# A four-mixer decoder block in split fp32: squares on GpSimd, moved value weights, a third half in two splits, a last block in unequal stores

## The chip, the cores and the metric

The kernel runs on one core of a Trainium2 chip. The metric is the device time of one execution in microseconds (us). A profiled execution shows the engines: TensorE (PE, with its weight loads as PEld), VectorE (DVE), ScalarE (ACT), GpSimd (POOL), and SyncE (SP), which here only starts DMAs.

## What is computed

One decoder layer on 256 tokens of width 2048, all in fp32:

```
h = rms_norm(x);  [qA|kA|vA|qB|kB|vB|qC|kC|vC] = h @ w_in       # 2048 x 6144
x = x + concat(diff_attention_A, moba_B, dilated_C) @ w_out     # 6 + 4 + 6 heads of 128
x = x + memory_cross_attention(rms_norm(x), rms_norm(mem), w_cq, w_ckv, w_co)
g, u = split(rms_norm(x) @ w_up);  g = causal_conv3(g) + conv_b
x = x + (silu(g) * u) @ w_down                                  # 2048 -> 2 x 5632 -> 2048
out = rms_norm(x)                                               # times g_final
```

`rms_norm(x)` is `x * rsqrt(mean(x * x) + 1e-6) * g`. Its sum of squares is what the change moves to another engine at the first norm.

## The kernel before, in words

x is kept transposed: 16 blocks of 128 features by 256 tokens in `xin`. Each fp32 operand of a large product is split into a high part, rounded to fp32r, and a low part (the rest), and a product is high x high + high x low + low x high. The norm's factor is applied after the product, so `hT` (x times the gain, high and low side by side, 512 columns a block) can be made at once and the sum of squares comes later.

Weights stream from HBM in **pieces** of 1 MB (`raw`, 4 buffers). A piece has two **halves** of 128 x 1024. For each half ScalarE copies the high part (`hi<-raw`, L142) and VectorE subtracts (`lo<-raw,hi`, L149); `hi` and `lo` have 5 buffers each. A half is split four halves ahead of its use; from the fifth buffer on, the split waits until TensorE is through with the buffer's last half. TensorE works half by half, in program order:

- `wstat_chunk`: a chunk of 512 output features, 8 halves. Weights are the stationary operand and `hT` moves: for each of 4 groups of 128 features and 2 blocks, a matmul of 512 columns (L295, high weights) and one of 256 (L302, low weights). A half has 8 such pairs. The four sums lie in four PSUM banks of the tag `acc`, which has 5. At the end `merge` (L354, L355) copies one side with ScalarE and adds the other with VectorE into `mg`; this frees the bank.
- `astat_chunk`: values for attention. Here the weights move (512 or 256 columns) and `hT` is stationary: L341, L342, L343.
- `down`: w_down, also with moving weights (L851, L852, L853). The last two of its 44 pieces wait until all else is summed and are then taken block by block of 512 output columns, so that a block's norm work lies beside the next block's matmuls.

Nothing schedules by itself: instructions stand on each engine in the order in which the code is written. `before(i, f)` and `after(i, f)` hang a piece of work ahead of or behind the matmuls of half i.

At the start SyncE and ScalarE issue the loads of x and of the first pieces in small parts, by turns (`load_x`, `load_block`, `load_half`); TensorE runs 24 transposes meanwhile. The squares of x are taken by ScalarE in four parts of 1024 columns (`square_part`, L223, after halves 5 to 8) and added by VectorE (L227). `norm_factors(10, "x")` folds them on VectorE ahead of half 10's splits (L236) and sums over partitions on TensorE behind half 10 (L241).

At the end (`down`, k = 43) each of the two token tiles goes block by block: add the sums to x (L900, L902), square and sum on ScalarE (L265), multiply by the gain (L873). Then the factor `rfin` (GpSimd, L915) scales: `finish` (L862 to L868) uses ScalarE, VectorE or GpSimd, and SyncE stores (L869). Block 3 of the second tile is split in two halves of 256 columns, the second in a bank of its own.

Of the kernel before, what the change touches and what calls it, by code (L numbers as in the profile page):

```python
# [20 lines left out]
NT = 2  # L21
# [41 lines left out]
def trunk(ctx, tc, x, mem, w_in, w_out, diff_lambda, rel_bias_table, w_cq, w_ckv, w_co, w_up, conv, w_down,  # L63
# [34 lines left out]


    class Piece:  # L100
        def __init__(self, srcs, mm, extra=None):
            self.srcs, self.mm, self.extra = srcs, mm, extra
            self.raw = None
            self.parts = [None, None]

# [25 lines left out]
    def load_half(p, h):  # L131
# [4 lines left out]
                       ap=[list(src.ap[0]), [src.ap[1][0], k], list(src.ap[2])])  # L136
        SP.dma_start(p.raw[:, h * HALF:(h + 1) * HALF].rearrange("p (k n) -> p k n", k=k), half)

    def split_hi(p, h):
        hi = wpool.tile([P, HALF], F32R, tag="hi", name="hi", bufs=NSPLIT)  # L140
        lo = wpool.tile([P, HALF], F32R, tag="lo", name="lo", bufs=NSPLIT)
        ACT.copy(hi, p.raw[:, h * HALF:(h + 1) * HALF])  # L142
        p.parts[h] = (hi, lo)
        if p.extra is not None and h == 0:
            p.extra[0]()
# [61 lines left out]
    def xblock(k):  # L207
        return xT[:, k, :]
# [5 lines left out]
    def square_part(i, key, c, src):  # L214

        st = {}

        def square():
            tag, bufs = ("v", 2) if key == "x" else ("sq", 1) if c else ("sqsum", 2)
            st["t"] = t = pools["att"].tile([P, NT, 512], F32, tag=tag, name="sq", bufs=bufs).rearrange("p t n -> p (t n)")  # L220
            if not c:
                squares[key] = t
            ACT.activation(t, src(), AF.Square)  # L223

        after(i, square)
        if c:
            before(i + 1, lambda: DVE.tensor_tensor(squares[key], squares[key], st["t"], op=ALU.add))  # L227
# [51 lines left out]
    def wstat_chunk(w, col0, src, evac, korder=tuple(range(KD)), bank=acc_tile, wide=True):  # L279


        accs = [None] * 4
        last = len(korder) // 4 - 1

        def mm(pi):
            def f(p, h):
                hi, lo = (a.rearrange("p (k n) -> p k n", k=2) for a in p.parts[h])
                if pi == 0 and h == 0:
                    accs[:] = [bank() for _ in range(4)]

# [13 lines left out]

                if cur[0] <= 2:
                    for f in (high, low):
                        for j in range(2):
                            for n in range(4):
                                f(n, j)
                    return  # L310
                for n in range(4):
                    for j in range(2):
                        high(n, j)
                        low(n, j)
                    if pi == last and h == 1:
                        evac(n, accs[n])
            return f

        for pi in range(last + 1):
            pieces.append(Piece(sources(w, korder[4 * pi:4 * pi + 4], col0, 512), mm(pi)))  # L320

    def astat_chunk(w, col0, ncol, src, evac, korder):

        accs = [None] * NT
        nk = 2 * HALF // ncol
        nkh = nk // 2
        last = len(korder) // nk - 1

        def mm(pi):
            def f(p, h):  # L330
                hi, lo = (a.rearrange("p (k n) -> p k n", k=nkh) for a in p.parts[h])
                for t in range(NT):
                    if pi == 0 and h == 0:
# [12 lines left out]
            return f  # L346

        for pi in range(last + 1):
            pieces.append(Piece(sources(w, korder[pi * nk:(pi + 1) * nk], col0, ncol), mm(pi)))

    def merge(a):

# [493 lines left out]
    def down_mm(p, k, h, t, n, c0=0, c1=512, own=None):  # L846
        hi, lo = p.parts[h]
        ah, al = (a[:, t * P:(t + 1) * P] for a in parts[k])
        o, first = (outs[t, 2 * h + n][:, c0:c1], 0) if own is None else (own, KF - TAIL)
        wh, wl = (a[:, n * 512 + c0:n * 512 + c1] for a in (hi, lo))  # L850
        PE.matmul(o, ah, wh, start=(k == first), stop=False)  # L851
        PE.matmul(o, ah, wl, start=False, stop=False)  # L852
        PE.matmul(o, al, wh, start=False, stop=(k == KF - 1))  # L853

    ss3 = small(10, "ss3", 1)
    fin = {}

    def finish(n, t, og, r):
        col = slice(n * 512, (n + 1) * 512)
        if t:  # L860
            if n < 2:
                ACT.activation(og[:, col], og[:, col], AF.Copy, scale=r)  # L862
            else:
                DVE.scalar_tensor_tensor(og[:, col], xtok(t, n), r, gfin["t"][:, col], op0=ALU.mult, op1=ALU.mult)
        elif n < 2:
            ACT.activation(og[:, col], og[:, col], AF.Copy, scale=r)
        else:
            POOL.tensor_scalar_mul(og[:, col], og[:, col], r)  # L868
        SP.dma_start(out[t * P:(t + 1) * P, col], og[:, col])  # L869

    def gained(og, t, n):
        col = slice(n * 512, (n + 1) * 512)
# [2 lines left out]
    def down(k):  # L875
        def f(p, h):
# [8 lines left out]
                        down_mm(p, k, h, t, n)  # L885
            elif k == KF - 1 and h == 1:
                done = None
                for t in range(NT):
                    og = wpool.tile([P, 2 * HALF], F32, tag="raw", name="raw", bufs=NRAW)
                    ms = small(2, "msf")  # L890
# [1 line left out]

                    parts_of = ((0, 0, 512), (1, 0, 512), (2, 0, 512)) + (((3, 0, 256), (3, 256, 512)) if t else ((3, 0, 512),))
                    for i, (n, c0, c1) in enumerate(parts_of):
                        own = any_tile()[:, :c1 - c0] if c0 else None
                        for kk in range(KF - TAIL, KF):
                            down_mm(fin[kk], kk, n // 2, t, n % 2, c0, c1, own)
                        xc = xtok(t, n)[:, c0:c1]
                        if own is None:
                            DVE.tensor_tensor(xtok(t, n), outs[t, n], xtok(t, n), op=ALU.add)  # L900
                        else:
                            DVE.tensor_tensor(xc, own, xc, op=ALU.add)  # L902
                        square_sum(xc, ss[:, i:i + 1], c1 - c0)
                        if done:
                            for m in ((2, 0), (3, 1), (), (), ())[i]:
                                finish(m, *done)
                        if not t or n < 2:
                            gained(og, t, n)
                    DVE.reduce_sum(ms[:, 0:1], ss[:, :3], axis=AX.X)
                    DVE.tensor_scalar(ms[:, 0:1], ms[:, 0:1], 1.0 / D, EPS, op0=ALU.mult, op1=ALU.add)  # L910
# [3 lines left out]
                    r = small(1, "rfin")  # L914
                    POOL.tensor_tensor(r, ms[:, 1:2], mhalf, op=ALU.pow)  # L915
                    done = t, og, r
                for n in (2, 0, 3, 1):
                    finish(n, *done)
        return f

    for k in range(KF):
# [20 lines left out]
                      bass.AP(tensor=src.tensor, offset=src.offset + k * src.ap[1][0],  # L942
                              ap=[list(src.ap[0]), list(src.ap[2])]))

    load_x(0, 2)
    load_block(ACT, pieces[0], 0)
    load_block(SP, pieces[0], 1)
    ACT.copy(small(1, "first", 1), mhalf)
    load_x(2, 2)
    load_half(pieces[0], 1)  # L950
    load_x(4, 2)
    load_half(pieces[1], 0)
    load_x(6, 2)
# [16 lines left out]
                f(xblock(k + j), MIX, lambda: hT["h"], k + j)  # L970

    def split(i):
        split_hi(pieces[i // 2], i % 2)
        split_lo(pieces[i // 2], i % 2)

    put_x(0)
    p = pieces[0]
    p.parts[0] = hi, lo = [wpool.tile([P, HALF], F32R, tag=t, name=t, bufs=NSPLIT) for t in ("hi", "lo")]
    for j in range(2):
        c = slice(j * 512, (j + 1) * 512)  # L980
        ACT.copy(hi[:, c], p.raw[:, c])
        DVE.tensor_tensor(lo[:, c], p.raw[:, c], hi[:, c].bitcast(F32), op=ALU.subtract)
    put_x(2)
    split(1)
    load(pieces[3])
    nload = 4

    for i in range(3):
        for j in range(2):
            after(i, lambda h=2 * i + j: (put_x(2 * h + 4), split(h + 2)))  # L990
    for c in range(4):
        square_part(c + 5, "x", c, lambda c=c: xpart(c))
    norm_factors(10, "x")
    mixed["t"] = buf1.tile([P, KD, 2 * S], F32R, tag="hT", name="hT")

# [85 lines left out]
```

## Time and profile before

| | us |
|---|---|
| median of 3 runs (1243.31 to 1245.57) | 1243.32 |
| the profiled execution's own time | 1244.53 |
| its span (first to last instruction) | 1242.7 |
| TensorE busy | 1229.7 |
| VectorE busy | 830.9 |
| ScalarE busy | 630.3 |
| GpSimd busy | 14.2 |

Times in the profile count from the span's start. A matmul's duration runs over the start of the next one, since matmuls are pipelined: the pace is read from the starts, the durations serve to compare equal shapes.

### The profile page before, as it was taken

The numbers are of one execution on the slowest core, as the hardware profiler recorded it, in microseconds if no ns is written. First come the engines' busy times: TensorE is split into PE (matmuls) and PEld (weight loads), VectorE is DVE, ScalarE is ACT, GpSimd is POOL, SyncE is SP. The second block draws the span as 40 slices with busy tenths as digits, with TensorE's granted clock in tenths as the row PEclk, the third lists the DMA queues.
The fourth block names the chain that finished last, engine by engine and source line by source line (L and its number), as shares of the span: only waits on it lengthen the run. The fifth ranks groups of instructions, "written<-read, shape, count | busy, mean of one in ns | idle before, by whom it ended". The sixth has DMA issues, their size and how long they took to land.

```text
span 1242.7 us, 17626 instructions
## 1 busy us (share of the span) xinstructions
PE 1229.7 (99%) x6934; PEld 1072.0 (86%) x6934; DVE 830.9 (67%) x1351; ACT 630.3 (51%) x981; POOL 14.2 (1%) x23
## 2 busy tenths in 40 slices
PE   8999999999999999999999999999999999999997
PEld 7888888988888899888888888888888888888885
DVE  7755667567568877776767768767677755554555
ACT  7445656556455656545444445444444544444444
POOL 0000000000000000000000000000000000000001
PEclk9999999999999999999999999999999999999998
DMA  9665554555566555565565565565656555555541
GB/s 345 209 195 190 175 178 163 184 168 173 177 216 218 170 169 166 202 206 173 169 203 183 190 198 178 182 203 190 197 176 203 185 188 204 180 192 203 180 160 68
DMA packets 104835, 233.26 MB, mean 188 GB/s; under 512 B 4208, under 2 KB 14768, under 8 KB 98992
## 3 DMA queue, kind: packets, MB, share of 16 engines
q1 hardware_dynamic: 104576, 231.85, 55.7%
q8 instruction: 54, 0.88, 0.3%
q10 hardware_dynamic: 144, 0.26, 0.1%
q14 instruction: 29, 0.24, 0.1%
q0 software_dynamic: 32, 0.02, 0.0%
HBM read 230.00 MB, written 2.12 MB: 187 GB/s over the span
## 4 chain that ended last, share of the span: by engine, by line
issue 58%; PE 37%; DVE 2%; DMA 1%; ACT 0%; POOL 0%; SPq 0%; POOLq 0%; DVEq 0%; ACTq 0%
PE acc L295 16%; PE acc L302 8%; PE acc L341 3%; PE acc L343 3%; PE acc L342 3%; DMA raw<-in_w_in 1%; PE at L401 1%; DVE lo L149 1%; PE at L420 0%; DMA xin<-in_x 0%; PE at L444 0%; PE acc L298 0%; PE acc L297 0%; DVE hT L197 0%; PE at L472 0%
## 5 line engine op out<-in xcount | busy, mean ns | idle before, releaser
L149 DVE TENSOR_TENSOR lo<-raw,hi 128x1024 fp32r<-128x1024 f32 x423 | 517.2, 1224 | 352.5 <-ACT hi L142 352.0
L142 ACT CAST hi<-raw 128x1024 fp32r<-128x1024 f32 x423 | 443.1, 1049 | 465.6 <-PE acc L295 273.3
L295 PE MATMUL acc<-hT,hi 128*128 128x512 f32 x1776 | 624.8, 394 | 2.5 <-DVE mg L355 1.9
L302 PE MATMUL acc<-hT,lo 128*128 128x256 f32 x1840 | 511.7, 280 | 0.0
L295 PEld LDWEIGHTS acc<-hT,hi 128*128 128x128 f32 x1776 | 334.0, 188 | 77.1 <-DVE mg L355 2.2
L302 PEld LDWEIGHTS acc<-hT,lo 128*128 128x128 f32 x1840 | 345.2, 188 | 0.3
L295 PE MATMUL at<-hT,hi 128*128 128x512 f32 x528 | 187.5, 392 | 0.0
L302 PE MATMUL at<-hT,lo 128*128 128x256 f32 x528 | 147.6, 280 | 0.0
L295 PEld LDWEIGHTS at<-hT,hi 128*128 128x128 f32 x528 | 99.2, 188 | 21.8
L302 PEld LDWEIGHTS at<-hT,lo 128*128 128x128 f32 x528 | 99.1, 188 | 0.0
L851 PE MATMUL acc<-hi,ah 128*128 128x512 f32 (+1 forms) x222 | 87.0, 392 | 0.0
L853 PE MATMUL acc<-hi,al 128*128 128x512 f32 (+1 forms) x222 | 86.6, 390 | 0.0
L852 PE MATMUL acc<-lo,ah 128*128 128x512 f32 (+1 forms) x222 | 85.7, 386 | 0.0
L341 PE MATMUL acc<-hi,hT 128*128 128x256 f32 (+1 forms) x224 | 75.0, 335 | 0.0
L343 PE MATMUL acc<-hi,hT 128*128 128x256 f32 (+1 forms) x224 | 73.9, 330 | 0.0
L342 PE MATMUL acc<-lo,hT 128*128 128x256 f32 (+1 forms) x224 | 73.8, 330 | 0.0
L788 ACT ACTIVATE y<-y 128x256 f32<-128x256 f32 x44 | 18.5, 419 | 66.4 <-DVE y L784 66.3
L851 PE MATMUL at<-hi,ah 128*128 128x512 f32 x132 | 52.0, 394 | 0.0
L853 PE MATMUL at<-hi,al 128*128 128x512 f32 x132 | 51.7, 392 | 0.0
L852 PE MATMUL at<-lo,ah 128*128 128x512 f32 x132 | 51.2, 388 | 0.0
L853 PEld LDWEIGHTS acc<-hi,al 128*128 128x128 f32 x222 | 41.7, 188 | 9.6
L852 PEld LDWEIGHTS acc<-lo,ah 128*128 128x128 f32 x222 | 41.7, 188 | 9.2
(159 smaller groups left out, 1005.0 us busy)
## 6 DMA issues: line engine op xcount, KB each, us to landing
raw<-in_w_up SPq DMA_DIRECT2D x88, 1024.0 KB, 5.1
raw<-in_w_in SPq DMA_DIRECT2D x45, 1024.0 KB, 5.2
raw<-in_w_down SPq DMA_DIRECT2D x44, 1024.0 KB, 4.9
raw<-in_w_out SPq DMA_DIRECT2D x12, 1024.0 KB, 5.2
raw<-in_w_ckv SPq DMA_DIRECT2D x8, 1024.0 KB, 5.3
raw<-in_w_out SPq DMA_DIRECT2D x8, 512.0 KB, 4.8
raw<-in_w_cq SPq DMA_DIRECT2D x4, 1024.0 KB, 5.3
raw<-in_w_co SPq DMA_DIRECT2D x4, 1024.0 KB, 5.3
```

The source lines that it names most:

```text
L142: ACT.copy(hi, p.raw[:, h * HALF:(h + 1) * HALF])
L149: DVE.tensor_tensor(lo, p.raw[:, h * HALF:(h + 1) * HALF], hi.bitcast(F32), op=ALU.subtract)
L295: PE.matmul(accs[n], w, x, start=(i == 0), stop=False)
L302: PE.matmul(accs[n][:, :S], lo[:, j, n * P:(n + 1) * P], src()[:, korder[i], :S], start=False, stop=(i == len(korder) - 1))
L341: PE.matmul(o, xh, hi[:, j, :], start=(i == 0), stop=False)
L342: PE.matmul(o, xh, lo[:, j, :], start=False, stop=False)
L343: PE.matmul(o, xl, hi[:, j, :], start=False, stop=(i == len(korder) - 1))
L401: PE.matmul(out, a[u], b[w], start=first and i == 0, stop=last and i == 2)
L788: after(cur[0] + 1 + n, lambda: ACT.activation(gate[k], gate[k], AF.Silu))
L851: PE.matmul(o, ah, wh, start=(k == first), stop=False)
L852: PE.matmul(o, ah, wl, start=False, stop=False)
L853: PE.matmul(o, al, wh, start=False, stop=(k == KF - 1))
```

## The change

Six things are changed.

1. **Squares of x.** The four squares of the first norm and their three additions become `POOL.tensor_tensor`, issued ahead of everything but the first setup. ScalarE and VectorE no longer have them.
2. **Rows of `hi` and `lo`.** Each buffer gets rows of 1280 elements instead of 1024. Value weights (`astat_chunk`) lie 56 elements (224 bytes) into the row, the others at its start. The room comes from a smaller DMA scratch, 4096 bytes instead of 16384, and so every tile lies elsewhere in SBUF.
3. **The start.** x's first two blocks are loaded one by one, the second half of the first piece in two loads, and the first two halves are split block by block; the third half's split is done in two parts of 512 columns.
4. **The order of the first half's matmuls.** Block 0 high and low, then block 1, instead of both highs first.
5. **The end, before the last block.** VectorE adds the sums of the second tile's block 3 without the last two pieces to x ahead of time, and both halves of that block get banks of their own.
6. **The last scalings and stores.** VectorE takes block 1 instead of ScalarE. The second tile's four stores have 256, 512, 768 and 512 columns instead of 512 each.

```
-        hi = wpool.tile([P, HALF], F32R, tag="hi", name="hi", bufs=NSPLIT)
-        lo = wpool.tile([P, HALF], F32R, tag="lo", name="lo", bufs=NSPLIT)
+        return [wpool.tile([P, HALF + 256], F32R, tag=t, name=t, bufs=NSPLIT)[:, p.shift:p.shift + HALF] for t in ("hi", "lo")]
...
-            pieces.append(Piece(sources(w, korder[pi * nk:(pi + 1) * nk], col0, ncol), mm(pi)))
+            pieces.append(Piece(sources(w, korder[pi * nk:(pi + 1) * nk], col0, ncol), mm(pi), shift=56))
...
+                DVE.tensor_tensor(xtok(1, 3), outs[1, 3], xtok(1, 3), op=ALU.add)
...
-                for n in (2, 0, 3, 1):
-                    finish(n, *done)
+                for n, c0, c1, send in ((2, 0, 256, 0), (0, 0, 512, 0), (2, 256, 512, None), (3, 0, 512, -256), (1, 0, 512, 0)):
+                    finish(n, *done, c0, c1, send)
...
-    load_x(0, 2)
+    load_x(0, 1)
     load_block(ACT, pieces[0], 0)
+    load_x(1, 1)
     load_block(SP, pieces[0], 1)
     ACT.copy(small(1, "first", 1), mhalf)
     load_x(2, 2)
-    load_half(pieces[0], 1)
+    load_block(SP, pieces[0], 2)
+    load_block(SP, pieces[0], 3)
...
-        square_part(c + 5, "x", c, lambda c=c: xpart(c))
+        t = pools["att"].tile([P, NT, 512], F32, tag="v", name="sq", bufs=2).rearrange("p t n -> p (t n)")
+        POOL.tensor_tensor(t, xpart(c), xpart(c), op=ALU.mult)
+        if c:
+            POOL.tensor_tensor(squares["x"], squares["x"], t, op=ALU.add)
...
-    nc = bacc.Bacc("TRN2", target_bir_lowering=False, num_devices=1)
+    nc = bacc.Bacc("TRN2", target_bir_lowering=False, num_devices=1, dynamic_dma_scratch_size=4096)
```

**Where instructions move.** VectorE around the first merges, before (`lo` are splits, `sq` squares, `mg` merges, each row with its line and the size of what it writes):

```order
16 L149 TENSOR_TENSOR lo<-raw,hi 128x1024 x4
17 L227 TENSOR_TENSOR sq<-sq 128x1024
18 L149 TENSOR_TENSOR lo<-raw,hi 128x1024
19 L355 TENSOR_TENSOR mg<-acc,mg 128x256 x4
20 L227 TENSOR_TENSOR sq<-sq 128x1024
21 L149 TENSOR_TENSOR lo<-raw,hi 128x1024
22 L227 TENSOR_TENSOR sq<-sq 128x1024
```

and the same place after the change:

```order
20 L152 TENSOR_TENSOR lo<-raw,hi 128x1024 x5
21 L358 TENSOR_TENSOR mg<-acc,mg 128x256 x4
22 L152 TENSOR_TENSOR lo<-raw,hi 128x1024 x2
23 L239 TENSOR_TENSOR sq<-sq 128x512
24 L239 TENSOR_TENSOR sq<-sq 128x256
```

The additions of squares are gone from VectorE; the folds of 512 and 256 columns stay and now read what GpSimd wrote. GpSimd's row from its last setup instruction (`ident`) to the first norm factor (`rcol_x`), after the change:

```order
10 masks.py:199 AFFINE_SELECT ident<-ident 128x128
11 L1024 TENSOR_TENSOR sq<-xin 128x1024 x2
12 L1026 TENSOR_TENSOR sq<-sq 128x1024
13 L1024 TENSOR_TENSOR sq<-xin 128x1024
14 L1026 TENSOR_TENSOR sq<-sq 128x1024
15 L1024 TENSOR_TENSOR sq<-xin 128x1024
16 L1026 TENSOR_TENSOR sq<-sq 128x1024
17 L193 TENSOR_TENSOR rcol_x<-ms_483,mhalf 128x2
```

Before, rows 11 to 16 were not there. VectorE at the very end, after the change (`xin<-acc` and `xin<-at` are sums, `msf` the norm's scalars, `raw` holds the result):

```order
994 L907 TENSOR_TENSOR xin<-at,xin 128x512
995 L868 TENSOR_SCALAR raw<-raw,rfin 128x512
996 L907 TENSOR_TENSOR xin<-at,xin 128x512
997 L907 TENSOR_TENSOR xin<-acc,xin 128x256 x2
998 L914 TENSOR_REDUCE msf<-ss_92 128x1
999 L915 TENSOR_SCALAR msf<-msf 128x1
1000 L917 SCALAR_TENSOR_TENSOR msf<-ss_92,msf 128x1
1001 L918 SCALAR_TENSOR_TENSOR msf<-ss_92,msf 128x1
1002 L864 SCALAR_TENSOR_TENSOR raw<-xin,rfin,gfin 128x256 x2
1003 L864 SCALAR_TENSOR_TENSOR raw<-xin,rfin,gfin 128x512 x2
```

Before, row 995 was the product with the gain, row 997 an addition of 512 columns and one of 256, and the last scalings were two of 512.

## Rows read from the trace of the kernel before

**Rows 1.** The page's head: span, then busy time, share, instructions.

```profile
span 1242.7 us, 17626 instructions
PE 1229.7 (99%) x6934; PEld 1072.0 (86%) x6934; DVE 830.9 (67%) x1351; ACT 630.3 (51%) x981; POOL 14.2 (1%) x23
```

**Rows 2.** Stretches: length, busy (instructions) by engine, granted clock, DMA share, GB/s.

```profile
31.50:34.85 3.35, 3.35 (x11) 2.87 (x12) 3.35 (x6) 1.87 (x2) 0.00 (x0) 0.50 1.01 334
```

**Rows 3.** Timeline of TensorE: start, length, line, operation, operands, [idle before <-releaser].

```profile
6.21 0.96 PE L295 MATMUL acc<-hT,hi 128*128 128x512 f32 x3 [0.64 <-DVE hT L197]
...
28.63 0.39 PE L295 MATMUL acc<-hT,hi 128*128 128x512 f32 x1
...
28.97 0.39 PE L295 MATMUL acc<-hT,hi 128*128 128x512 f32 x1
...
31.36 0.71 PE L295 MATMUL acc<-hT,hi 128*128 128x512 f32 x1 [1.88 <-DVE mg L355]
...
32.08 0.63 PE L295 MATMUL acc<-hT,hi 128*128 128x512 f32 x1
```

**Rows 4.** Timeline of VectorE ahead of the first merges.

```profile
23.85 4.85 DVE L149 TENSOR_TENSOR lo<-raw,hi 128x1024 fp32r<-128x1024 f32 x4
28.62 1.22 DVE L227 TENSOR_TENSOR sq<-sq 128x1024 f32<-128x1024 f32 x1
29.75 1.22 DVE L149 TENSOR_TENSOR lo<-raw,hi 128x1024 fp32r<-128x1024 f32 x1
30.89 1.41 DVE L355 TENSOR_TENSOR mg<-acc,mg 128x256 f32<-128x256 f32 x4
```

**Rows 5.** Timeline of ScalarE in the start phase.

```profile
10.81 0.91 ACT L194 ACTIVATE hT<-xin 128x256 fp32r<-128x256 f32 x2
...
20.83 1.05 ACT L142 CAST hi<-raw 128x1024 fp32r<-128x1024 f32 x1 [2.69 <-DMA raw<-in_w_in]
...
25.45 1.06 ACT L223 ACTIVATE sq<-xin 128x1024 f32<-128x1024 f32 x1
26.41 1.03 ACT L142 CAST hi<-raw 128x1024 fp32r<-128x1024 f32 x1
```

**Rows 6.** Groups by shape: count, then busy us, mean ns, idle us before.

```profile
L302 PE MATMUL acc<-hT,lo 128*128 128x256 f32 x1840 | 511.7, 280 | 0.0
...
L851 PE MATMUL acc<-hi,ah 128*128 128x512 f32 x218 | 85.9, 394 | 0.0
...
L852 PE MATMUL acc<-lo,ah 128*128 128x512 f32 x218 | 84.6, 388 | 0.0
...
L341 PE MATMUL acc<-hi,hT 128*128 128x512 f32 x96 | 38.6, 402 | 0.0
...
L342 PE MATMUL acc<-lo,hT 128*128 128x512 f32 x96 | 37.8, 393 | 0.0
L341 PE MATMUL acc<-hi,hT 128*128 128x256 f32 x128 | 36.4, 284 | 0.0
L342 PE MATMUL acc<-lo,hT 128*128 128x256 f32 x128 | 36.1, 282 | 0.0
```

**Rows 7.** Timeline of GpSimd at the end.

```profile
1230.85 3.59 POOL L868 TENSOR_SCALAR raw<-raw,rfin 128x512 f32<-128x512 f32 x2
1235.55 0.57 POOL L915 TENSOR_TENSOR rfin<-msf,mhalf 128x1 f32<-128x1 f32 x1 [1.12 <-DVE msf L913]
```

**Rows 8.** Timeline of VectorE at the end.

```profile
1224.79 0.69 DVE L873 TENSOR_TENSOR raw<-xin,gfin 128x512 f32<-128x512 f32 x1
...
1232.09 0.69 DVE L873 TENSOR_TENSOR raw<-xin,gfin 128x512 f32<-128x512 f32 x1
...
1236.16 1.41 DVE L864 SCALAR_TENSOR_TENSOR raw<-xin,rfin,gfin 128x512 f32<-128x512 f32 x2 [0.69 <-POOL rfin L915]
```

**Rows 9.** Timeline of TensorE: the column sums of the squares.

```profile
40.66 0.50 PE L241 MATMUL at<-ones,sq 128*128 128x1 f32 x4
```

**Rows 10.** The same view as Rows 2, for the last stores.

```profile
1237.75:1240.00 2.25, 0.00 (x0) 0.00 (x0) 0.00 (x0) 0.00 (x0) 0.00 (x0) 0.50 1.03 351
```

More of the change, by code (lines that the diff above doesn't have):

```diff
@@ L100, in trunk, with __init__ @@
     class Piece:
-        def __init__(self, srcs, mm, extra=None):
-            self.srcs, self.mm, self.extra = srcs, mm, extra
+        def __init__(self, srcs, mm, extra=None, shift=0):
+            self.srcs, self.mm, self.extra, self.shift = srcs, mm, extra, shift
             self.raw = None
@@ L137, in load_half, with part_tiles @@
         SP.dma_start(p.raw[:, h * HALF:(h + 1) * HALF].rearrange("p (k n) -> p k n", k=k), half)
+    def part_tiles(p):
+        return [wpool.tile([P, HALF + 256], F32R, tag=t, name=t, bufs=NSPLIT)[:, p.shift:p.shift + HALF] for t in ("hi", "lo")]
     def split_hi(p, h):
-        hi = wpool.tile([P, HALF], F32R, tag="hi", name="hi", bufs=NSPLIT)
-        lo = wpool.tile([P, HALF], F32R, tag="lo", name="lo", bufs=NSPLIT)
+        hi, lo = part_tiles(p)
         ACT.copy(hi, p.raw[:, h * HALF:(h + 1) * HALF])
@@ L218, in square @@
         def square():
-            tag, bufs = ("v", 2) if key == "x" else ("sq", 1) if c else ("sqsum", 2)
+            tag, bufs = ("sq", 1) if c else ("sqsum", 2)
             st["t"] = t = pools["att"].tile([P, NT, 512], F32, tag=tag, name="sq", bufs=bufs).rearrange("p t n -> p (t n)")
@@ L305, in f @@
                 if cur[0] <= 2:
[L306 to L309, printed above, removed]
+                    for j, f in (((0, high), (0, low), (1, high), (1, low)) if cur[0] == 0 else
+                                 ((0, high), (1, high), (0, low), (1, low))):
+                        for n in range(4):
+                            f(n, j)
                     return
@@ L852, in down_mm, with finish @@
         PE.matmul(o, ah, wl, start=False, stop=False)
-        PE.matmul(o, al, wh, start=False, stop=(k == KF - 1))
+        PE.matmul(o, al, wh, start=False, stop=k == KF - 1 or (own is None and (t, 2 * h + n, k) == (1, 3, KF - TAIL - 1)))
     ss3 = small(10, "ss3", 1)
     fin = {}
[L858 to L865, printed above, removed]
+    def finish(n, t, og, r, c0=0, c1=512, send=0):
+        col = slice(n * 512 + c0, n * 512 + c1)
+        if t and n:
+            DVE.scalar_tensor_tensor(og[:, col], xtok(t, n)[:, c0:c1], r, gfin["t"][:, col], op0=ALU.mult, op1=ALU.mult)
+        elif n == 0:
             ACT.activation(og[:, col], og[:, col], AF.Copy, scale=r)
+        elif n == 1:
+            DVE.tensor_scalar_mul(og[:, col], og[:, col], r)
         else:
             POOL.tensor_scalar_mul(og[:, col], og[:, col], r)
-        SP.dma_start(out[t * P:(t + 1) * P, col], og[:, col])
+        if send is not None:
+            col = slice(n * 512 + send, n * 512 + c1)
+            SP.dma_start(out[t * P:(t + 1) * P, col], og[:, col])
     def gained(og, t, n):
@@ L894, in f @@
                     for i, (n, c0, c1) in enumerate(parts_of):
-                        own = any_tile()[:, :c1 - c0] if c0 else None
+                        own = any_tile()[:, :c1 - c0] if (t, n) == (1, 3) else None
                         for kk in range(KF - TAIL, KF):
@@ L899, in f @@
                         if own is None:
-                            DVE.tensor_tensor(xtok(t, n), outs[t, n], xtok(t, n), op=ALU.add)
-                        else:
-                            DVE.tensor_tensor(xc, own, xc, op=ALU.add)
+                            own = outs[t, n][:, c0:c1]
+                        DVE.tensor_tensor(xc, own, xc, op=ALU.add)
                         square_sum(xc, ss[:, i:i + 1], c1 - c0)
@@ L906, in f @@
                                 finish(m, *done)
-                        if not t or n < 2:
+                        if not t or n < 1:
                             gained(og, t, n)
@@ L972, in split, with put_high, put_low @@
     def split(i):
+        if i == 2:
+            p = pieces[1]
+            p.parts[0] = hi, lo = part_tiles(p)
+            for c in (slice(0, 512), slice(512, HALF)):
+                ACT.copy(hi[:, c], p.raw[:, c])
+                DVE.tensor_tensor(lo[:, c], p.raw[:, c], hi[:, c].bitcast(F32), op=ALU.subtract)
+            return
         split_hi(pieces[i // 2], i % 2)
         split_lo(pieces[i // 2], i % 2)
-    put_x(0)
+    def put_high(k):
+        high(xblock(k), MIX, lambda: hT["h"], k)
+    def put_low(k):
+        low(xblock(k), MIX, lambda: hT["h"], k)
     p = pieces[0]
[L978 to L984, printed above, removed]
+    for h in range(2):
+        p.parts[h] = hi, lo = part_tiles(p)
+        if h:
+            put_high(2)
+            put_high(3)
+        for j in range(2):
+            k = 2 * h + j
+            c = slice(j * 512, (j + 1) * 512)
+            r = p.raw[:, h * HALF + j * 512:h * HALF + (j + 1) * 512]
+            if h == 0:
+                put_high(k)
+            n = 2 if k == 0 else 1
+            for i in range(n):
+                w = 512 // n
+                ACT.copy(hi[:, j * 512 + i * w:j * 512 + (i + 1) * w], r[:, i * w:(i + 1) * w])
+            put_low(k)
+            DVE.tensor_tensor(lo[:, c], r, hi[:, c].bitcast(F32), op=ALU.subtract)
     load(pieces[3])
@@ L991, in trunk @@
     for c in range(4):
-        square_part(c + 5, "x", c, lambda c=c: xpart(c))
+        t = pools["att"].tile([P, NT, 512], F32, tag="v", name="sq", bufs=2).rearrange("p t n -> p (t n)")
+        POOL.tensor_tensor(t, xpart(c), xpart(c), op=ALU.mult)
+        if c:
+            POOL.tensor_tensor(squares["x"], squares["x"], t, op=ALU.add)
+        else:
+            squares["x"] = t
     norm_factors(10, "x")
```

## The prediction

> **What bounds the kernel now.** I read the page's busy line first, then the queries by stretch and by time for the start and the end, then the groups of matmuls by shape. TensorE is busy 1229.7 of 1242.7 us [rows 1]; the reader is to see that a microsecond on VectorE, ScalarE or GpSimd counts only where TensorE waits for it, and that there are three ways to gain: shorter matmuls, fewer waits, a shorter end. The waits are nearly all in one place. At 28.97 us a pair of matmuls starts, pairs follow each other every 0.34 us, and the next one starts at 31.36, so 31.36 - 28.97 - 0.34 = 2.05 us are lost [rows 3]. The next pair takes 0.72 instead of 0.34 us, since the granted clock is 0.50 (the 1.2 GHz level) for the 3.35 us behind the pause [rows 2, 3]: half of 3.35, 1.7 us, is lost again. Together 3.7 us.
>
> What TensorE waits for there is an accumulator of the first chunk, freed by VectorE's `mg` additions. They start at 30.89, behind four splits (23.85 on), an addition of squares (28.62) and another split (29.75), one closely after the other [rows 4]. On ScalarE two squares of 1.06 us stand among the casts that these splits need [rows 5].
>
> **The change part by part.**
>
> *Squares on GpSimd.* ScalarE loses four squares, VectorE three additions of 1.22 us. VectorE's row before the merges is then five splits and no addition: the fifth split takes the addition's place at 28.62, the first merge the place of the split at 29.75, 1.14 us ahead of 30.89 [rows 4]. TensorE went on at 31.36 and so goes on 1.14 earlier, at 30.22; it wants the bank at 29.31, so 0.9 us of the wait stay. The casts are no hindrance: without the square of 25.45 the cast of 26.41 can only come earlier [rows 5]. Whether the clock drops behind a wait of 0.9 us is not shown; the one of 0.64 at 6.21 was followed by matmuls at full pace, three in 0.96 us [rows 3], so I take it that it does not, and the 1.7 are won too. Sum -2.8; bounds -3.7 (no wait at all) and -1.1 (the clock drops just the same), and on the other side the first two rivals below.
>
> *The price on GpSimd.* Seven operations of 128x1024 with two inputs. The nearest rows: two of 128x512 with one input took 3.59 us, 1.8 each, of which 0.57 is about what an operation on one column takes [rows 7]. So 1024 columns cost 0.57 + 2 x 1.23 = 3.0 us if the second input is free, and 5.5 if it costs as much as the first. I take 3.5. Six of the seven come after blocks 4 to 7 of x, the last of which ScalarE reads at 10.81 [rows 5], so the sum is ready near 10.8 + 6 x 3.5 = 32. VectorE folds it in two additions (some 1.2 us, by 0.69 for 512 columns [rows 8] and half as many more), and TensorE's column sums, in order behind the eleventh half, come at 40.66 now [rows 9] and 2.8 us earlier then, at 37.9: 36.7 less the fold. The limit is (36.7 - 10.8) / 6 = 4.3 us an operation. Cost 0 with that cover. VectorE's new wait at the fold holds back splits of halves that TensorE reads four halves later, so it alone costs nothing.
>
> The Trainium skill ("GPSIMD Engine Reference", section 3.1, Elementwise) gives 4497 ns for an addition of 2048 columns of fp32; an estimate from it is some 2.3 to 2.5 us for 1024, with which the sum would be ready near 26 us; no run here shows it yet.
>
> *Finer loads and another order at the start.* TensorE's first real matmul, at 6.21 [rows 3], can come some 0.7 us earlier, since the first block of x is sent alone. But ScalarE waits until 20.83 for the weights of the seventh half [rows 5], its cast of 1.05 and its split of 1.2 end near 23.1, and TensorE is there already: 6.21 + 6 halves of 8 pairs at 0.345 = 22.8. The bytes ahead of that load are the same, so what is won at 6 us is waited for at 23. I take 0; bounds -0.3 and +0.5 (the stepwise order, with casts of one block that TensorE waits for one by one).
>
> *Value weights.* 288 matmuls of 512 columns and 384 of 256 (96 and 128 on each of three lines [rows 6]). The 512s last 402 ns on L341 and 393 on L342 (L343 is like L342), 396 on the mean; those of w_down, of equal shape but at other places in SBUF, 394 and 388 on L851 and L852 (L853 lies between them), 391 on the mean: 288 x 5 ns = 1.4 us. The 256s last 284 and twice 282, against 280 on L302: 2.7 x 384 = 1.0. If the moved rows run like the others, 2.4 us are won; I take 2.0, since the 402 holds some matmuls that followed a pause. No row shows a matmul on weights 224 bytes further. Bounds: all like L852 (388), -3.4; all like L341, +2.1. The other weights keep their place in a row, but rows get 1024 bytes longer and every buffer lies elsewhere; the three lines of w_down differ by 6 ns with nothing but operands to tell them apart, so 1056 of them could go 3 ns either way, 3.2 us. I take 0.
>
> *The end.* The first half of the last block no longer waits for an addition over 512 columns, and ScalarE has one scaling less between its sums: the last sum comes 0.2 us sooner. VectorE scales all but one quarter: 1.41 us for two of 512 columns now [rows 8], with two of 256 more about 2.3, so its last product is ready 0.7 later. But the stores, not the products, set the end: from 1237.75 to 1240 the queues move 351 GB/s, DMA share 1.03 [rows 10], and a first store of 128 KB can go 0.3 us sooner. About -0.5; bounds -1.0 (all of 0.2 and 0.3, and no gap) and +0.7 (the last store waits for VectorE). The first block's new VectorE scaling shares its time with GpSimd's and is within these bounds.
>
> **Sum.** -2.8 - 2.0 - 0.5 = -5.3. The profiled execution took 1244.53 us (span 1242.7 and 1.8 around it), so 1239.2 for it; the median of the three runs before lies 1.2 lower, at 1243.32, hence the forecast of 1238.0.
>
> **Rivals.**
>
> *GpSimd holds VectorE back (slower).* Both read SBUF, and every split has two SBUF inputs. If a GpSimd operation keeps the path until it ends, each split that meets one waits. In the stretch from 23.85 on, where VectorE has hardly a gap [rows 4], GpSimd would be at work all the time; two or three waits of 3 us each stand ahead of the merges. TensorE then waits 0.9 us and that delay, the clock falls for 1.7, and what is won elsewhere is 2.5: at two waits 0.9 + 6 + 1.7 - 3.7 - 2.5 = +2.4, 1245.7; at three 1248.7. It decides from a delay of 3.6 us. Against it: at 1232.09 VectorE multiplied two SBUF tensors in 0.69 us, while GpSimd's first scaling had run since 1230.85, and the same product alone, at 1224.79, also took 0.69 [rows 7, 8]. The Trainium skill ("SBUF — State Buffer", Who interferes with whom) has this rule, an exclusive lock in which the one that comes second blocks fully; by it the trace disagrees on VectorE's side, in this one instance. Chance 0.10.
>
> *The squares come late.* Past 4.3 us an operation TensorE waits at the column sums: at 5.5 the sum is ready at 43.8, a wait of 7.1 us and 1.7 for the clock, against 5.3 won: 1246.8. From 4.9 us on it is slower than before. For it: the bounds 3.0 and 5.5 lie on either side of the limit. Chance 0.12, two thirds of it slower, the rest no change.
>
> *Most of it given back (no change).* The clock drops behind the shorter wait, so the start gives 1.1, or 0.5 if GpSimd slows the splits a little; the values keep their 393 to 402 ns, and the end gives 0.3: 1242.0 to 1242.5. For it: no row shows the new place of the values, or a wait of 0.9 us in full work. Against it: the full pace behind the wait at 6.21 [rows 3]. Chance 0.18, a quarter of it faster by a little over 0.2%.
>
> **How the numbers follow.** The forecast has 0.60, with its own range 1235.2 to 1240.6 (start -1.6 to -3.7, values -1.0 to -3.4, end -0.1 to -1.0, all ends together left out). What a measurement can tell here is 0.2%, 2.5 us. Faster 0.60 + 0.04 = 0.64; slower 0.10 + 0.08 = 0.18; no change 0.18. The range that leaves out two in ten: 1234.4 (beyond it the unshown gain of w_down) to 1244.5 (beyond it the first two rivals).
>
> **What would show it.** Right: no idle stretch over 1 us on TensorE between 28 and 32 us and a granted clock of 1.00 through 35; the first `mg` addition near 29.75; GpSimd's last addition before 36 us; splits still at 1.22 us; L344 to L346 (the old L341 to L343) near 391 and 280 ns; the last store's data complete some 0.5 us sooner after the last matmul. Wrong: splits that last or wait over 2 us between 10 and 35 us (the first rival); TensorE idle before the column sums (the second); value matmuls at 393 to 402 as before, or w_down's durations changed (my terms of 2.0 and 0).

## The result, and the profile after

| | us | against the kernel before |
|---|---|---|
| forecast | 1238.0 (1234.4 to 1244.5) | faster |
| kernel before, 4 runs beside it | 1244.05 (1243.31 to 1245.57) | |
| changed kernel, 4 runs | 1252.15 (1251.75 to 1252.86) | ratio 1.0067, interval 1.0052 to 1.0082 |

The change made the kernel slower by 0.5 to 0.8%; the forecast had the wrong sign, and the time lies outside its range. Two executions far outside all others, 4752.02 us of the kernel before and 1454.63 us of the run with the squares one half later in it, are left out of every comparison below. The span grew from 1242.7 to 1250.0 us. The page's head after, with its busiest row of matmuls (columns as in [rows 1] and, for the last line, group | busy, mean ns | idle before, releaser):

```profile
span 1250.0 us, 17646 instructions
...
PE 1230.7 (98%) x6934; PEld 1072.7 (86%) x6934; DVE 841.4 (67%) x1353; ACT 626.5 (50%) x978; POOL 30.3 (2%) x30
...
L305 PE MATMUL acc<-hT,lo 128*128 128x256 f32 x1840 | 512.6, 280 | 7.5 <-DVE lo L152 4.5
```

TensorE did as many matmuls in nearly the same busy time [rows 1]; what grew is idle time, from 13.0 to 19.3 us, and one group has 7.5 of it, on VectorE's account. GpSimd has 30.3 us instead of 14.2. VectorE is busier by 10.5 us although three additions of 1.22 us went away: its instructions lasted longer.

To find the place, I compared the start of each matmul in the two traces (both have 6934). The changed kernel is 0.05 us ahead at the first real one, 12.9 us late at the hundredth, 9.2 late at the column sums (49.86 us; 40.66 before [rows 9]), still 9.2 late at the first value matmul, 7.9 at the last, 8.0 at the kernel's last matmul, 7.3 at the span's end. So the start lost 9.2, the values gave 1.3, the end gave 0.8. All of the loss falls between 7 and 30 us. VectorE there (start, length, line, operation, operands, [idle before]; several rows left out):

```profile
7.15 2.03 DVE L200 SCALAR_TENSOR_TENSOR hT<-xin,hT 128x256 fp32r<-128x256 f32 x1
9.11 0.68 DVE L1014 TENSOR_TENSOR lo<-raw,hi 128x512 fp32r<-128x512 f32 x1
...
10.71 2.51 DVE L200 SCALAR_TENSOR_TENSOR hT<-xin,hT 128x256 fp32r<-128x256 f32 x2
13.14 5.15 DVE L985 TENSOR_TENSOR lo<-raw,hi 128x512 fp32r<-128x512 f32 x2
18.21 4.60 DVE L200 SCALAR_TENSOR_TENSOR hT<-xin,hT 128x256 fp32r<-128x256 f32 x2
22.74 3.35 DVE L152 TENSOR_TENSOR lo<-raw,hi 128x1024 fp32r<-128x1024 f32 x1
...
26.81 1.21 DVE L152 TENSOR_TENSOR lo<-raw,hi 128x1024 fp32r<-128x1024 f32 x1
```

and GpSimd:

```profile
6.75 2.15 POOL L1024 TENSOR_TENSOR sq<-xin 128x1024 f32<-128x1024 f32 x1 [5.40 <-DMA xin<-in_x]
10.73 2.20 POOL L1024 TENSOR_TENSOR sq<-xin 128x1024 f32<-128x1024 f32 x1 [1.83 <-DMA xin<-in_x]
13.01 2.43 POOL L1026 TENSOR_TENSOR sq<-sq 128x1024 f32<-128x1024 f32 x1
...
22.61 2.40 POOL L1026 TENSOR_TENSOR sq<-sq 128x1024 f32<-128x1024 f32 x1
```

The reader is to lay the two lists on one axis. A split of 512 columns takes 0.68 us at 9.11 and 2.6 at 13.14, a split of 1024 takes 3.35 at 22.74 and 1.21 at 26.81. GpSimd is at work from 10.73 to 25.01 almost without a gap, and in that time VectorE gets one operation through for each of GpSimd's. With the one at 7.15 that makes seven, and together they last 12.9 us longer than usual. Before 10.73 (but for 7.15, beside GpSimd's first) and after 25.01 every length is the usual one. TensorE's waits, each on what VectorE was late with:

```profile
16.05 0.73 PE L305 MATMUL acc<-hT,lo 128*128 128x256 f32 x4 [1.52 <-DVE lo L985]
...
18.35 0.73 PE L305 MATMUL acc<-hT,lo 128*128 128x256 f32 x4 [1.57 <-DVE lo L985]
...
20.93 0.77 PE L298 MATMUL acc<-hT,hi 128*128 128x512 f32 x1 [1.85 <-DVE hT L200]
...
26.15 0.58 PE L305 MATMUL acc<-hT,lo 128*128 128x256 f32 x1 [4.45 <-DVE lo L152]
```

And the clock (columns as in [rows 2]):

```profile
5.00:14.10 9.10, 8.99 (x48) 7.38 (x47) 8.98 (x11) 8.06 (x17) 5.44 (x3) 1.00 1.03 386
...
19.53:29.77 10.24, 4.39 (x13) 3.42 (x14) 10.24 (x9) 2.79 (x4) 5.33 (x3) 0.50 0.47 154
```

During the third of those waits the granted clock fell to 0.50 (the 1.2 GHz level) for 10.24 us. From start to start the four steps are 1.91, 1.84, 2.12 and 5.22 us where one matmul's step is about 0.2: 10.2 us lost. From 26.15 to 29.77 TensorE works at half pace, which costs another 1.8. With the 0.5 it was late by 14 us already, that makes 12.5 of the 12.9. The pause and half clock that the kernel before had near the first merges [rows 2, 3] no longer occur, and the lag falls from 12.9 to 9.2: TensorE comes there that much later, and VectorE has caught up (its two splits ahead of the merges wait 1.08 and 1.55 us for their casts).

### The profile page after: what moved, and what is told of

Same layout as the page of the kernel before. It is cut to its first block, busy times and chain, and to the rows that moved or that the text cites. A ratio compares the mean times of both kernels' runs of the same rounds, so it can differ in the third digit from the quotient of the medians.

```text
span 1250.0 us, 17646 instructions
## 1 busy us (share of the span) xinstructions
PE 1230.7 (98%) x6934; PEld 1072.7 (86%) x6934; DVE 841.4 (67%) x1353; ACT 626.5 (50%) x978; POOL 30.3 (2%) x30
## 3 DMA queue, kind: packets, MB, share of 16 engines
HBM read 230.00 MB, written 2.12 MB: 186 GB/s over the span
## 4 chain that ended last, share of the span: by engine, by line
issue 58%; PE 38%; DVE 2%; DMA 1%; POOL 0%; SPq 0%; ACT 0%; POOLq 0%; DVEq 0%; ACTq 0%
PE acc L298 16%; PE acc L305 9%; PE acc L344 3%; PE acc L346 3%; PE acc L345 3%; DMA raw<-in_w_in 1%; PE at L404 1%; DVE lo L152 1%; DVE hT L200 1%; PE at L423 0%; PE at L447 0%; PE acc L301 0%; PE acc L300 0%; PE at L475 0%; POOL raw L870 0%
```

## The experiments

Two theories stood after this reading. A: GpSimd's operations hold VectorE's back, whoever needs their result. B: the finer loads and the stepwise splits of the start cost it. "Lag" below is how much later TensorE starts the column sums (or their half) than at 40.66 us in the kernel before; a ratio is that of the times, with its interval. The profiled execution that gives the 40.66 has the half clock of [rows 2], 1.7 us by the prediction's sum; and one kernel profiled twice, the changed kernel with its squares one half later (below), has lags of -0.5 and -1.8. So a lag of one or two microseconds decides nothing.

**The squares back.** The changed kernel, its squares on ScalarE and VectorE as before:

```
-        POOL.tensor_tensor(t, xpart(c), xpart(c), op=ALU.mult)
...
+        square_part(c + 5, "x", c, lambda c=c: xpart(c))
```

> The changed kernel with the four squares back on ScalarE and their additions on VectorE, as in the kernel before; all else as changed. Theory A (GpSimd's two-input operations hold VectorE's splits back): the 9.2 us that the start lost are gone, the pause ahead of the first merges is back, so the start stands within 0.5 us of the kernel before; the values keep 1.2 and the end 0.7 us: about 1.9 us under the kernel before, near 1242.1. Theory B (the finer loads and the stepwise splits of the start cost it): the start stays some 9 us late, near 1252. VectorE's splits of 1024 columns last 1.22 us under A, over 2 us under B.

1241.44 us, ratio 0.9990 (0.9980 to 0.9999); lag -1.1 us, splits at 1.22 us. Six of its ten executions took 1241.21 to 1241.45 us, four 1242.51 to 1243.03. A holds, B falls: before the first merges TensorE is 0.6 us behind the kernel before, and 0.5 and 0.6 us in two runs below that have the old loads and splits ("by itself" and "one input"), so the new ones cost nothing that can be told.

**The squares alone.** The kernel before with only the squares moved:

```
-        square_part(c + 5, "x", c, lambda c=c: xpart(c))
+        POOL.tensor_tensor(t, xpart(c), xpart(c), op=ALU.mult)
...
```

> The kernel before with nothing but the squares and their additions on GpSimd. Theory A (GpSimd's two-input operations hold VectorE's splits back): the column sums come some 9 us later than in the kernel before, as in the changed one, and the time is near 1253 to 1254. Theory B (the finer loads and the stepwise splits cost it): only the pause ahead of the merges goes, near 1241.2.

1254.08 us, ratio 1.0087 (1.0071 to 1.0103); lag +10.1. The one part makes the whole loss, and more than the others give back.

**Whose result it is.** The kernel before, whole, and beside it seven GpSimd products that nobody reads (the smaller DMA scratch makes room for them):

```
+    dum = cst.tile([P, 1024], F32, name="dum")
+    for c in (0, 1, 1, 2, 2, 3, 3):
+        POOL.tensor_tensor(dum, xpart(c), xpart(c), op=ALU.mult)
```

> The kernel before, its squares left on ScalarE and VectorE, with a smaller DMA scratch (4096 bytes) and seven GpSimd products of 128x1024 beside it at the place of the changed kernel's, two inputs each, into a tile that nobody reads. Theory A, as a lock (a two-input operation of GpSimd and one of VectorE exclude each other until they end, whoever needs the result): VectorE gets about one operation through for each of the seven, its splits take up to 3.4 us, the column sums come near 50 us instead of 40.7, time near 1253 to 1254. Rival (what held the start back was waiting for the squares, not their execution): nothing moves, near 1243.

One run: 1252.8 us beside 1243.04 for the kernel before; lag +8.2. So it is not a wait for the squares. VectorE, then GpSimd, then the longest wait of TensorE:

```profile
10.03 1.21 DVE L149 TENSOR_TENSOR lo<-raw,hi 128x1024 fp32r<-128x1024 f32 x1
11.17 4.14 DVE L197 SCALAR_TENSOR_TENSOR hT<-xin,hT 128x256 fp32r<-128x256 f32 x2
15.24 2.91 DVE L149 TENSOR_TENSOR lo<-raw,hi 128x1024 fp32r<-128x1024 f32 x1
18.07 4.14 DVE L197 SCALAR_TENSOR_TENSOR hT<-xin,hT 128x256 fp32r<-128x256 f32 x2
22.14 2.91 DVE L149 TENSOR_TENSOR lo<-raw,hi 128x1024 fp32r<-128x1024 f32 x1
24.97 0.87 DVE L197 SCALAR_TENSOR_TENSOR hT<-xin,hT 128x256 fp32r<-128x256 f32 x2
```

```profile
10.77 13.19 POOL L995 TENSOR_TENSOR dum<-xin 128x1024 f32<-128x1024 f32 x6 [2.00 <-DMA xin<-in_x]
```

```profile
25.10 0.58 PE L302 MATMUL acc<-hT,lo 128*128 128x256 f32 x1 [4.01 <-DVE lo L149]
```

Six GpSimd operations from 10.77 to 23.96, and six of VectorE from 11.17 to 25.05, by turns, with the same two durations each time: 2.1 where an `hT` takes 0.48, 2.9 where a split takes 1.21.

**Half the size.** Fourteen products of 512 columns instead of seven of 1024 (`dum[:, o:o + 512]`, o = 0 and 512):

> As d2_two_inputs, with fourteen products of 512 columns instead of seven of 1024. Lock that changes hands after each operation: VectorE gets fourteen operations through beside the fourteen instead of seven, each waits 1.1 to 1.3 us instead of 2.2, so the delay of the column sums falls to about half, 4 to 6 us: near 1248. If what counts is GpSimd's whole busy time: 10 us as before, near 1253.

One run: 1249.57 us; lag +4.8, against 8.2. GpSimd:

```profile
10.40 16.03 POOL L996 TENSOR_TENSOR dum<-xin 128x512 f32<-128x512 f32 x11 [0.89 <-DMA xin<-in_x]
```

VectorE, and TensorE's longest wait:

```profile
11.24 2.44 DVE L197 SCALAR_TENSOR_TENSOR hT<-xin,hT 128x256 fp32r<-128x256 f32 x2
13.60 2.06 DVE L149 TENSOR_TENSOR lo<-raw,hi 128x1024 fp32r<-128x1024 f32 x1
...
17.95 2.06 DVE L149 TENSOR_TENSOR lo<-raw,hi 128x1024 fp32r<-128x1024 f32 x1
```

```profile
20.06 0.58 PE L302 MATMUL acc<-hT,lo 128*128 128x256 f32 x1 [2.59 <-DVE lo L149]
```

An `hT` takes 1.2 us now (two in 2.44), a split 2.06: each waits for one GpSimd operation, and a shorter one holds it back for some 0.8 us and not 1.7. But twice as many are held back. Summed over its operations of the start, VectorE works 10.7 us longer here (fourteen operations) and 11.6 with the larger products (seven), so the turns cost it nearly the same. What fell is TensorE's share. It waits longest for the same split in both runs: that one ends at 25.05 there, after all seven long turns, and at 20.01 here, after nine of the fourteen short ones; of the other five TensorE waits for hardly any (0.46 us at 27.89). The half clock falls with it, from 10.24 us to 3.41. So the lag came out as expected, though not because the turns had become cheaper in sum.

That VectorE and GpSimd hold each other back is what the first rival described. The Trainium skill ("SBUF — State Buffer", Who interferes with whom) calls the ports that the two engines share an exclusive lock, and says that a VectorE instruction with two SBUF inputs contends with a GpSimd instruction that reads SBUF; the traces of this pair agree, with 2.1 and 2.9 us for VectorE's operations beside products of 1.95 to 2.75 us.

**One input on GpSimd.** The same place, but a scaling by a column:

```
-        POOL.tensor_tensor(dum, xpart(c), xpart(c), op=ALU.mult)
+        POOL.tensor_scalar_mul(dum, xpart(c), mhalf)
```

> As d2_two_inputs, but the seven GpSimd operations are scalings by a column, with one 128x1024 input each. If only the two-input form takes the path (as the end of the kernel before suggested, where VectorE's product kept 0.69 us beside a scaling): VectorE's splits stay at 1.22 us, column sums near 40 us, time near 1243. If any GpSimd operation on SBUF takes it: splits of over 2 us and column sums near 50 us again. One operation near 3.0 us by the two scalings of 512 columns at the end of the kernel before.

One run: 1243.29 us beside 1243.04; lag -1.3, without a half clock at the merges. The smaller DMA scratch and the moved tiles are the same here as in the two runs with products, so the loss is not theirs. GpSimd and VectorE:

```profile
11.18 26.34 POOL L995 TENSOR_SCALAR dum<-xin,mhalf 128x1024 f32<-128x1024 f32 x6 [0.95 <-DMA xin<-in_x]
```

and the fourth of these six by itself:

```profile
22.77 6.82 POOL L995 TENSOR_SCALAR dum<-xin,mhalf 128x1024 f32<-128x1024 f32 x1
```

```profile
11.43 2.04 DVE L149 TENSOR_TENSOR lo<-raw,hi 128x1024 fp32r<-128x1024 f32 x1
13.39 0.87 DVE L197 SCALAR_TENSOR_TENSOR hT<-xin,hT 128x256 fp32r<-128x256 f32 x2
14.19 1.21 DVE L149 TENSOR_TENSOR lo<-raw,hi 128x1024 fp32r<-128x1024 f32 x1
15.32 1.65 DVE L197 SCALAR_TENSOR_TENSOR hT<-xin,hT 128x256 fp32r<-128x256 f32 x2
...
23.46 3.49 DVE L149 TENSOR_TENSOR lo<-raw,hi 128x1024 fp32r<-128x1024 f32 x3
```

A scaling takes 4.2 us on the mean, from 2.95 to 6.82. Beside five of the seven a single VectorE operation, which starts 0.2 to 1.5 us after the scaling, is longer by 0.8 us (2.04 for 1.21, 1.65 for a pair of 0.87); the rest of the scaling goes by beside normal VectorE operations. Beside the one of 6.82 us VectorE's three splits from 23.46 on keep their length, and only the next one is longer, by 0.3; that it is then GpSimd that waits is likely, but not shown. So my estimate of 3.0 us for a scaling held for the shortest alone, and the two forms differ in what they hold. The Trainium skill's rule ("SBUF — State Buffer", Who interferes with whom) speaks of any GpSimd instruction that reads SBUF; here the trace agrees with it for a part of the scaling only.

**No shift.** The kernel of the first experiment with `shift=0` instead of `shift=56`:

> The kernel of e1_no_gpsimd (squares back on ScalarE and VectorE) with the value weights at the start of their longer rows instead of 224 bytes further. If the 224 bytes shortened the value matmuls: the value phase, from the first to the last of its lines, is 1.3 us longer again, 395.65 instead of 394.34 us, and the 512-column matmuls of high weights on the first line are back near 402 ns. If the longer rows or the other places in SBUF did it: 394.3 us as in e1_no_gpsimd.

One run: 1241.90 us. From the first to the last value matmul of that phase it takes 395.62 us, against 394.34 with the shift and 395.65 in the kernel before (394.32 to 394.37 in the six profiles with the shift, 395.62 to 395.66 in the seven without). So the 224 bytes are worth 1.3 us, and longer rows and other places by themselves nothing. The groups without the shift:

```profile
L344 PE MATMUL acc<-hi,hT 128*128 128x512 f32 x96 | 38.6, 402 | 0.0
...
L344 PE MATMUL acc<-hi,hT 128*128 128x256 f32 x128 | 36.4, 284 | 0.0
L345 PE MATMUL acc<-lo,hT 128*128 128x256 f32 x128 | 36.1, 282 | 0.0
```

**The addition ahead of the merges, by itself.** The kernel before with its squares one half later, on their old engines:

```
-        square_part(c + 5, "x", c, lambda c=c: xpart(c))
+        square_part(c + 6, "x", c, lambda c=c: xpart(c))
```

> The kernel before with its squares one half later and nothing else: the step of the prediction that removes the addition ahead of the merges, by itself. If it is worth what the prediction says: 2.8 us, near 1241.2, first merge near 29.75 us and clock 1.00 throughout 31 to 35 us. If the clock falls behind the shorter pause: 1.1 us, near 1242.9. If the squares merely push the later splits into TensorE's way: no gain, near 1244.

1242.96 us, ratio 0.9998 (0.9988 to 1.0008): no gain that can be measured. VectorE:

```profile
24.02 4.62 DVE L149 TENSOR_TENSOR lo<-raw,hi 128x1024 fp32r<-128x1024 f32 x4
29.25 1.23 DVE L149 TENSOR_TENSOR lo<-raw,hi 128x1024 fp32r<-128x1024 f32 x1 [0.61 <-ACT hi L142]
30.39 1.41 DVE L355 TENSOR_TENSOR mg<-acc,mg 128x256 f32<-128x256 f32 x4
```

ScalarE and TensorE:

```profile
27.22 1.06 ACT L223 ACTIVATE sq<-xin 128x1024 f32<-128x1024 f32 x1
28.18 1.03 ACT L142 CAST hi<-raw 128x1024 fp32r<-128x1024 f32 x1
```

```profile
30.86 0.50 PE L295 MATMUL acc<-hT,hi 128*128 128x512 f32 x1 [0.90 <-DVE mg L355]
```

The merge comes at 30.39 and not at 29.75: the fifth split, put in the addition's place, waits 0.61 us for its cast, and this cast stands right behind a square that is still on ScalarE here. TensorE still waits 0.90 us (1.88 in [rows 3]), and the clock stays at 1.00. The time, 1242.96, is near the 1242.9 that was expected if the clock fell; it did not fall, so that this figure fits is luck.

**The same in the changed kernel**, in two comparisons:

> The changed kernel with the squares on ScalarE and VectorE, each one half later than in the kernel before, so that VectorE has no addition ahead of the first merges. Theory A: the start gains what the prediction gave it, 2.8 us (2.05 of a pause shrinks to about 0.9 and the clock keeps 1.00), the values 1.2, the end 0.7: near 1239.3. If the clock falls behind the shorter pause just the same, near 1241.0. Theory B (loads and stepwise splits cost the start 9 us): near 1249.

> The kernel of e5_squares_later once more, for a tighter interval beside e11_merges_first on the same chip: 1241.4, which is 1.7 us under the kernel before.

1241.52 us, ratio 0.9982 (0.9972 to 0.9992), and 1241.13, ratio 0.9980 (0.9971 to 0.9989): faster than the kernel before, but within 0.3 us of the first experiment, where the squares stand one half earlier. What has gone are that experiment's longer executions: none of these 21 took over 1242.2 us. The 2.8 us are not there.

**The merges first.** The kernel above with the last split of half 7 written behind the merges:

```
+        if i == 7:
+            pieces[i // 2].mm(pieces[i // 2], i % 2)
         for p, h in new:
             split_lo(p, h)
-        pieces[i // 2].mm(pieces[i // 2], i % 2)
+        if i != 7:
+            pieces[i // 2].mm(pieces[i // 2], i % 2)
```

> The kernel of e5_squares_later with the first merges written ahead of VectorE's last split before them (half 7 alone). If VectorE's row is all that the pause ahead of the first merges came from: the one step of TensorE over 0.8 us between 28 and 32 us (1.18 to 1.95 us in the runs so far) goes, the clock stays at 1.00 in every execution, and the time is 0.8 to 1.5 us under e5_squares_later: near 1240.2. If the merges' other half on ScalarE, behind casts, is as late: no gain, near 1241.4.

1241.60 us, ratio 0.9985 (0.9976 to 0.9994): the pause of the merges is gone and the time is no better. TensorE:

```profile
30.10 0.50 PE L298 MATMUL acc<-hT,hi 128*128 128x512 f32 x1 [0.24 <-DVE mg L358]
```

and, from the same view later on:

```profile
39.26 0.61 PE L244 MATMUL at<-ones,sq 128*128 128x1 f32 x4 [1.24 <-DVE sq L239]
```

TensorE is early at the column sums now and waits there for VectorE's fold of the squares.

**The sums a half later**, too:

```
-        after(i, total)
-        before(i + 1, column)
+        j = i + (key == "x")
+        after(j, total)
+        before(j + 1, column)
```

> The kernel of e11_merges_first with the column sums of the first norm on TensorE one half later (behind half 11 instead of half 10), and what follows them. In e11_merges_first TensorE waited 1.24 us there for VectorE's folds. If that wait was the one of the merges, handed on: no step over 0.8 us is left in TensorE's start, and the time falls by 1.2 us, to about 1240.4; it is then under e5_squares_later (1241.1) by 0.7. If the wait is handed on again (to the splits of the halves behind, or to the factor's turn): no gain, near 1241.5.

1239.93 us (1239.40 to 1240.22), ratio 0.9971 (0.9959 to 0.9983), lag -2.8 at the same half: faster than both kernels, the best of this study. No step of TensorE between 6 and 60 us is over 0.8 us. Its first wait on the merges, and the stretches (columns as in [rows 2]):

```profile
30.09 0.50 PE L299 MATMUL acc<-hT,hi 128*128 128x512 f32 x1 [0.28 <-DVE mg L359]
```

```profile
28.00:36.00 8.00, 7.72 (x45) 6.53 (x44) 7.07 (x10) 6.61 (x11) 0.00 (x0) 1.00 0.96 336
36.00:45.00 9.00, 9.00 (x57) 8.05 (x56) 6.70 (x9) 4.87 (x6) 0.71 (x1) 1.00 0.78 248
```

## Why the prediction was wrong, step by step

**The step that failed: "Cost 0 with that cover".** I asked of the squares on GpSimd only when their result would be ready, and it was ready in time (25.01 us; the limit was 37.9 less the fold). The cost was on VectorE's row: its seven operations that met GpSimd's lasted 12.9 us longer, and the time grew by 10.7 us (the changed kernel against the run with the squares back) and 10.9 (the squares alone against the kernel before). The mechanism stood among the rivals, with 0.10. I argued it away with one row, the product of 0.69 us at 1232.09 beside GpSimd's scaling [rows 7, 8]. That row could not carry this: the scaling has one input, and it had begun 1.24 us earlier. The run with scalings shows that beside a scaling at most one VectorE operation is longer, by 0.8 us, and the next ones not at all. The rival was also priced too low, at two or three waits in the stretch from 23.85 on: seven operations met VectorE's, from 7.15 us on and six of them without a gap from 10.7 on, where I had looked only for when x arrives; by 25.01 they were through.

**"GpSimd would cost 3.0 to 5.5, I take 3.5."** It took 2.0 to 2.7 us in the changed kernel, below both ends. I had scaled from the one-input scaling, and that form is the slower one: for 1024 columns 4.2 us on the mean (2.95 at the least) with one input, 2.2 with two. The estimate from the Trainium skill ("GPSIMD Engine Reference", section 3.1, Elementwise), 2.3 to 2.5, was the better one. The second rival (squares late) fell with this.

**"-2.8" for the addition ahead of the merges: mis-sized.** The changed kernel cannot show this term: there is no pause at the merges and the clock is 1.00 through 35 us, but TensorE gets there 12.9 us late. The kernel before with its squares a half later shows the mechanism, a wait of 0.90 us for 1.88 and no half clock, and yet a time that is 0.2 us shorter and not 2.8. First, 1.7 of it was the half clock, and by the times the kernel before does not always have that: of 24 executions in one comparison 20 took 1242.76 to 1243.87 us and four 1244.42 to 1244.83, with mean granted clocks of 0.997 to 0.998 and 0.996 to 0.997 (in two others 7 of 21 and 2 of 10 took 1244.45 or more). The profile I read, of an execution of 1244.53, is of the second kind; none of the first was profiled, but the run with scalings, with the same order at the merges, waits 1.53 us there and keeps a clock of 1.00. I took 1.2 us off to come to the median, and those 1.2 were, by this, the half clock: counted twice. Second, the wait of 0.9 was forecast for a merge at 29.75, and it came at 30.39, behind a cast. Whether "the casts are no hindrance" failed stays open: that cast followed a square on ScalarE, and the change leaves none there. Third, what was left of the pause was handed on to the column sums, as the run with the merges first shows, and came out only when these moved as well: from 1241.13 to 1239.93, 1.2 us for the pause, between two comparisons in which the kernel before took 1243.22 and 1243.07.

**"-2.0" for the values: mis-sized.** It is -1.3, and the 224 bytes alone make it. The groups after:

```profile
L344 PE MATMUL acc<-hi,hT 128*128 128x512 f32 x96 | 38.3, 399 | 0.0
...
L345 PE MATMUL acc<-lo,hT 128*128 128x512 f32 x96 | 37.8, 394 | 0.0
L344 PE MATMUL acc<-hi,hT 128*128 128x256 f32 x128 | 36.1, 282 | 0.0
L345 PE MATMUL acc<-lo,hT 128*128 128x256 f32 x128 | 35.7, 279 | 0.0
```

Against [rows 6] the 256-column groups lost 0.3 to 0.4 us each, 1.1 together, as forecast (1.0). The 512-column ones did not come down to w_down's 391 ns: 38.6 to 38.3 us on the first line, no less on the others. Equal shape was not enough to carry a duration from w_down over.

**Terms that held.** The start's finer loads: 0; the first real matmul came at 6.16 us (6.21 before), and between 5.48 and 6.44 in the other runs. w_down: unchanged, 394 and 388 ns on its first two lines as in [rows 6]. The end: -0.5 forecast; from the last matmul's start to the span's end it was 9.35 us before and 8.58 after, -0.8. VectorE's last products are ready at 1246.0, 4.6 us after the last matmul's start (4.2 before), and the stores still end sooner:

```profile
1243.82 2.20 DVE L864 SCALAR_TENSOR_TENSOR raw<-xin,rfin,gfin 128x256 f32<-128x256 f32 x4 [0.69 <-POOL rfin L920]
```

So the sum is +9.2 at the start (forecast -2.8), -1.3 (-2.0) and -0.8 (-0.5): 7.1, against a span longer by 7.3, all of it beside the profiled execution before with its half clock.

## What to carry to other kernels

Before a two-input operation goes to GpSimd, look at what VectorE does beside it: if that row is two-input operations on SBUF without gaps, each GpSimd operation costs VectorE a turn of about its own length, whoever needs the result and however early it is ready. Operations of half the size did not make the turns cheaper in sum here; they only moved some of them to where TensorE did not wait. A row that is to speak against such a cost must be of the same form and must overlap the other operation from its start. A wait that an order change removes was won here only when the next reader of the same late engine had been moved too; and if the profiled execution differs from the median, find out what it has that the others lack before a term of the sum is taken from it.

## What the runs showed of the hardware

- GpSimd's scaling of 128x1024 by a column (one SBUF tensor in) took 4.2 us on the mean (2.95 to 6.82), its product of two inputs 2.2 (1.95 to 2.75).
- A product shut a two-input operation of VectorE out until it ended (longer by 1.5 to 2.2 us for a product of 1024 columns, by about 0.8 for one of 512); a scaling lengthened at most one, by about 0.8 us. Why they differ is open. VectorE operations with one SBUF input were not tried beside products.
- Weights that move through TensorE from 224 bytes further into a row shorten a 256-column matmul by 2 to 3 ns and leave a 512-column one nearly as it was (402 to 399 ns on one line, 393 to 394 on another). Which addresses are good was not tried.
- The granted clock fell to 0.50 for 10.24 us during the third of three pauses of 1.5 to 1.9 us close together, and for 3.41 us after one of 1.88 in the profiled execution of the kernel before; it stayed at 1.00 after one of 1.67 in the run with the squares back and one of 1.53 in the run with scalings.
